# Memory gates that may be projected early, memory values for two token blocks side by side, attention values for two query blocks a group

## The chip, the cores and the metric

The kernel runs on one core of one Trainium2 chip. The metric is the device time of one execution in microseconds (us), as the median of several runs; lower is better. One profiled execution of the same program gives the page and the trace that are read here.

## The reference, cut to what matters

Two layers act on a stream x of 512 tokens by 1024 channels. Each layer has four branches that read the same x: a recurrence (RWKV), a causal attention with low-rank latents (MLA), a convolution, and a cross-attention into 256 memory tokens. Each branch output of width 512 is multiplied by its own gate, projected to 1024 channels and merged under a second set of gates.

```python
h = x @ w_in[l]                                   # all projections of x, gates included
# causal attention, 8 heads of 64, swept in query blocks of 128
s = where(key <= query, (q @ k.T) * scale, -1e30); o = softmax(s) @ v
# memory cross-attention, 4 heads of 128
kv = mem @ w_mem_kv                               # 256 memory tokens: keys and values
y_mem = (softmax(xq @ k_mem.T * scale) @ v_mem) * silu(xg)
...
merged = sum(sigmoid(merge + b) * (y_branch @ w_o_branch), over branches)
x = layer_norm(alpha * x + merged @ w_out)
```

## The kernel before, in words

A product in full precision is made of three matmuls (`mm3`): each operand is split into a high and a low half, and high by low, high by high and low by high are summed in one PSUM bank. A projection of x (`project`) has eight steps over the 1024 input channels, three matmuls of 128 by 512 each, so 24 matmuls. Its weight comes as one DMA of 512 KB, and ScalarE and VectorE split it into halves before TensorE can use it.

Nothing of the order is decided on the chip. While the program is built, the class `Plan` keeps an estimated clock for every engine and lays the instructions out in that order. There are two sources of work. One is a *stream* of items, each with weights to load and a body to run; one item runs at a time and the next waits for it. The other is a set of *tasks* (attention blocks, convolution taps, units of the recurrence), each of which goes on as soon as the planner believes its data to be there. When a task is due it goes first; otherwise the stream gives the next piece; when neither can go on, the planner moves TensorE's clock forward, and the chip will idle there.

- `pick` chooses the next item of the stream: the first in list order whose `ready` holds, and if there is none, the first whose `soon` holds. `prefetch` calls it while fewer than four half-weights are held and fewer than two raw weights are in flight (`LOOK = 4`, `WR = 2`). Weight DMAs are issued by SyncE in that order.
- The list of a layer has latents (`pl`), convolution (`ps_glu`, `ps_val`), memory queries (`ps_xq`), the recurrence's inputs, then four gates and four merge items for each branch. Branch 3 is the memory cross-attention: its gates are `ps_xg` 0 to 3, its merge items give `ps_m` and `po`. A gate item is ready when the branch output that it multiplies exists (`ymem[i]`); a merge item may be taken "soon" once all four gates of its branch have been picked (`picked[n] == 4`), and its body then holds the stream until the four gated outputs `Y[n]` are there. `xq` 2 and 3 are ready when `ymem` 0 and 1 exist.
- Memory values (`pmv`, function `vpart`, by the helper `narrow`): two items a layer, each for 256 value channels. One item computes token block 0 over all eight steps, then token block 1 over the same eight steps; the weights are held through both. `w125` and `w126` are such weights, at the seam of the layers, where layer 0's output is transposed (`xT`), turned into layer 1's x (`xf`, `xh`, `xl`) and read by the latents (`pl`).
- MLA: `pair_item` projects the queries and keys of two heads (`pq`, `pk`), `heads` moves them by DMA to the layout `qT`, `kT`, and `pair` starts eight jobs (`mla_block`), four query blocks for each of the two heads, three in flight at most. A job computes scores (`ms`), maximum (`nmm`), exponential (`mP`), scaling, transposes by TensorE (`mt`) and a copy by ScalarE (`mPT`, four buffers). When both heads of one query block have their `mPT`, their products with the values (`mo`) are issued as one group. These use a 128 by 64 piece of the array, where almost all other matmuls use 128 by 128.
- `Plan.shape` charges the planner's TensorE clock 98 ns whenever the piece of the array changes, and 108 ns more for a return to 128 by 128 unless the matmul is f16. A task that yields "small" waits up to 3 us (`GATHER`) so that small matmuls come together.
- Two PSUM banks belong to the stream (`pp`), two to tasks that use a bank briefly (`pa`), and four to MLA or the recurrence (`pg`).

The recurrence of a layer begins when the four pairs of MLA are done; merge items of the branches fill TensorE beside it.

Of the kernel before, what the change touches and what calls it, by code (L numbers as in the profile page):

```python
# [10 lines left out]
F32 = mybir.dt.float32  # L11
# [14 lines left out]
APART = 150  # L26
ORDER = ["z0", "m0", "m1", "z2", "m2", "m4", "z3", "m3", "m5"]
LOOK = 4
GATHER = 3000.0
WR = 2  # L30
WH = 6
# [40 lines left out]
class Plan:  # L72
# [56 lines left out]
    def shape(self, k, m, quick=False):  # L129


        if (k, m) != self.cut:
            self.clk["PE"] += 98.0 if self.cut != (128, 128) or (k, m) != (128, 128) else 0.0
            if (k, m) == (128, 128) and not quick:
                self.clk["PE"] += 108.0
            self.cut = k, m
            self.cuts += 1
            self.tiled = self.clk["PE"]
# [190 lines left out]
def build(ctx: ExitStack, tc: tile.TileContext, A, out, log, slots, dbg=None):  # L329
# [42 lines left out]
    pp = pool(2, name="pp", space=PSUM)  # L372
    pa = pool(2, name="pa", space=PSUM)
# [141 lines left out]
    both = set()  # L515
# [32 lines left out]
    def free(n=1):  # L548
        wlive["hl"] -= n
# [66 lines left out]
    def narrow(get, cols, blocks, name, lhs, after):  # L616

        wb = []
        for b in range(blocks):
            ps = pp.tile([128, cols], F32, tag="pp", name=f"{name}{b}")  # L620
            for k in range(8):
                if len(wb) <= k // 2:
                    wb.append((yield from get()))
                h, lo = wb[k // 2]
                c = slice(cols * (k % 2), cols * (k % 2) + cols)
                xh, xl = lhs(k, b)
                mm3(ps, xh, xl, h[:, c], lo[:, c], k == 0, k == 7)
                if b == blocks - 1 and k % 2:
                    free()
                if k in (1, 3, 5):  # L630
                    yield
            yield from after(b, ps)
# [26 lines left out]
    def memory_items(l):  # L659

        ms = []
        res = {}

        def load(pool):
            raws = []
            for i in range(4):
                raws.append(u(f"mr{i}_{l}"))
                DMA(raws[i], A["memT"][:, 512 * i:512 * i + 512])
            hl = [[pool(f"mem{n}{i}_{l}") for n in "hl"] for i in range(4)]
            for x in "kv":  # L670
                res[x] = [[u(f"{x}m{n}{i}_{l}", 512, F32R) for n in "hl"] for i in range(2)]
            for i, (h, lo) in enumerate(hl):
                plan.due(raws[i])
                yield
                yield from split(h, lo, raws[i])
                for b in range(2):
                    c = slice(256 * b, 256 * b + 256)
                    ms.append((h[:, c], lo[:, c]))

        def keep(x, i, b, ps):  # L680
            h, lo = (y[:, 256 * b:256 * b + 256] for y in res[x][i])
            return split(h, lo, ps)

        def keys(h):
            def run(get):
                ps = yield from project(get, ms, f"mk{h}_{l}", 256)
                yield from keep("k", h // 2, h % 2, ps)
                yield
            return run

        def vpart(b):
            def after(i, ps):
                yield from keep("v", i, b, ps)
                if b == i == 1:
                    MEM[l] = (res["k"], res["v"])
                yield

            def run(get):
                return narrow(get, 256, 2, f"pmv{b}{l}", lambda k, i: [x[:, 128 * i:128 * i + 128] for x in ms[k]], after)
            return run  # L700

        its = [([(A["w_mk"][l, h], (512, 512))], keys(h)) for h in range(4)]
        its += [([(A["w_mv"][l, b, kh], (512, 512)) for kh in range(2)], vpart(b)) for b in range(2)]
        return load, its, lambda: len(ms) == 8
# [9 lines left out]
    def layer_items(l):  # L714
# [14 lines left out]
        def item(blocks, run, ready=None, picked=None, soon=None):  # L729
            items.append((blocks, run, ready, picked, soon))  # L730

        def ch_item(i, name, after, ready=None, picked=None):

            def run(get):
                ps = yield from project(get, X[l], name + t_)
                after(ps)
                yield
            item([(A["w_ch"][l, i], (512, 512), False, True)], run, ready, picked)

        picked, adds = [0] * 4, [0] * 8  # L740


        if l == 0:
# [775 lines left out]
        def pair(hh, qT, kT, there):  # L1519
            yield lambda: L["turn"] == hh and len(there) == 8  # L1520
            mo, = yield from pg.take([128, 512], f"mo{hh}" + t_)
            plan.t = max(plan.t, *(plan.done[x][0] for x in there + [f"qTpe{hh}1" + t_]))
            yield
            left = [4]
            for i in range(4):
                both = [None, None]
                for h in range(2):
                    while L["jobs"] == 3:
                        yield lambda: L["jobs"] < 3
                    L["jobs"] += 1  # L1530
                    plan.spawn(mla_block(hh, h, i, (qT[h], kT[h]), mo, both, left))
                    yield
            L["turn"] += 1

        def mla_block(hh, h, i, T, mo, both, left):


            n = 128 * i + 128
            dg = slice(128 * i, n)
            q = f"{hh}{h}{i}" + t_  # L1540
            ps, = yield from pg.take([128, n], "ms" + q)
            mm3(ps, *(x[:, dg] for x in T[0]), *(x[:, 0:n] for x in T[1]), True, False)
            MM(ps[:, dg], idb, causal, start=False, stop=True)
            yield
            P = m("mP" + q, 512, "mP", 3)[:, 0:n]
            nm, sm = st("nmm" + q, 1), st("smm" + q, 1)
            V.tensor_reduce(out=nm, in_=ps, axis=AX.X, op=ALU.max, negate=True)
            yield
            S.activation(P, ps, AF.Exp, bias=nm, accum_out=sm)
            pg.free()  # L1550
            yield
            V.reciprocal(sm, sm)
            V.tensor_scalar(out=P, in0=P, scalar1=sm, scalar2=None, op0=ALU.mult)
            yield
            ps, = yield from pg.take([128, n], "mt" + q)
            for kb in range(i + 1):
                TR(ps[:, 128 * kb:128 * kb + 128], P[:, 128 * kb:128 * kb + 128])
            yield
            PT = m("mPT" + q, 512, "mPT", 4)[:, 0:n]
            S.copy(PT, ps)  # L1560
            pg.free()
            both[h] = PT
            L["jobs"] -= 1
            if both[1 - h] is None:
                return
            yield "small"
            for kb in range(i + 1):
                for half, x in zip(range(2), both):
                    MM(mo[HALF[half], dg], vtok[kb][:, 128 * hh + 64 * half:128 * hh + 64 * half + 64], x[:, 128 * kb:128 * kb + 128], start=kb == 0, stop=kb == i)
            left[0] -= 1  # L1570
            if left[0] == 0:
                L["pairs"] += 1
                yield
                yo = u(f"mo{hh}" + t_)
                S.copy(yo, mo)
                pg.free()
                ymla.append(yo)
                if len(ymla) == 4:
                    close_phase()
                    L["mla"] = True  # L1580
# [8 lines left out]
        def gate_items(n, base, name, ready, ys, res, op):  # L1589
            for i in range(4):  # L1590
                def after(ps, i=i):
                    t = sp.tile([128, 512], F32, tag="tg", name=f"t{name}{i}" + t_)
                    S.activation(t, ps, AF.Tanh, scale=0.5)
                    g = u(f"{name}{i}" + t_)
                    V.scalar_tensor_tensor(out=g, in0=t, scalar=1.0, in1=ps, op0=ALU.add, op1=ALU.mult)

                    def fin():
                        yield lambda: ready(i)
                        y = ys[i]
                        op(i, y, g)  # L1600
                        if i == 0:
                            dump(f"y_{name}{l}", y)

                        yield lambda: turn(n)
                        plan.due(y)
                        yield
                        res[i] = yield from halves(f"y{name}{i}", t_, y)
                    plan.spawn(fin())
                def count():
                    picked[n] += 1  # L1610
                ch_item(base + i, f"{name}{i}", after, lambda i=i: ready(i) or n == 0 and added[2] == 8, count)

        def fin(d):
            merged[d] = yield from halves(f"mg{d}", t_, merged[d])
# [462 lines left out]
```

## Time and profile before

| | |
|---|---|
| median of 3 runs | 1527.68 us (1526.68 to 1528.75) |
| the profiled execution | 1528.06 us, its span 1526.3 us |
| TensorE (PE) busy | 1503.4 us, 98% of the span |
| VectorE (DVE) busy | 1079.8 us, 71% |
| ScalarE (ACT) busy | 701.8 us, 46% |
| mean granted TensorE clock | 0.995 |

The span runs from the first to the last instruction; the profiled execution's own time holds 1.8 us more around it. A row of the timeline gives start, duration, engine, line, operation, tiles, shape and count, and in brackets the idle time of the engine ahead of it with what released it. Matmuls overlap, so the price of one is read from start to start, not from its duration. `w147h` is the high half of the stream's weight number 147. A window's row gives the length, then for each engine the busy time and the number of instructions, then the granted TensorE clock (1.00 is full speed), the share of the DMA engines that is busy, and GB/s.

### The profile page before, as it was taken

What the parts mean: (1) busy time and instruction counts of PE and PEld (TensorE: products, weight loads), DVE (VectorE), ACT (ScalarE), POOL (GpSimd) and SP (SyncE); (2) the same over time, 40 slices, a digit from 0 to 9 for tenths busy, and PEclk for the clock granted to TensorE, in tenths of its full rate; (3) what the DMA queues carried; (4) which work ended last, traced back from release to release, by engine and by line L of the source; (5) the groups of instructions that cost most, each with busy time, mean ns of one, the idle gap of its engine ahead of it and who ended that gap; (6) DMA issues with size and microseconds to landing.
All of it is one profiled execution on the core that took longest, in us unless ns stands there. A gap on an engine that the chain in (4) does not pass through costs nothing.

```text
span 1526.3 us, 30171 instructions
## 1 busy us (share of the span) xinstructions
PE 1503.4 (98%) x11942; PEld 1235.8 (81%) x11942; DVE 1079.8 (71%) x2330; ACT 701.8 (46%) x1586; POOL 234.1 (15%) x558
## 2 busy tenths in 40 slices
PE   9999999999999999999999979999999999999997
PEld 9987788877777777888998867788777777778886
DVE  6788887888757774445655878887887777654756
ACT  6546564444345443343364455634544454433330
POOL 0000000334314330000000000000543243300001
PEclk9999999999999999999999999999999999999999
DMA  6351422222222223323343143332222222234222
GB/s 226 126 158 61 107 95 97 74 89 74 72 85 62 76 86 126 110 97 138 115 134 129 53 123 83 109 97 72 88 70 80 86 62 74 86 123 170 97 99 81
DMA packets 69838, 152.13 MB, mean 100 GB/s; under 512 B 24256, under 2 KB 25792, under 8 KB 69696
## 3 DMA queue, kind: packets, MB, share of 16 engines
q1 hardware_dynamic: 69696, 150.20, 31.1%
q8 instruction: 94, 1.54, 0.4%
q14 instruction: 48, 0.39, 0.1%
HBM read 133.39 MB, written 5.24 MB: 91 GB/s over the span
## 4 chain that ended last, share of the span: by engine, by line
PE 94%; DVE 3%; ACT 2%; DMA 1%; issue 0%; SPq 0%; POOL 0%; DVEq 0%; ACTq 0%
PE ps_m L349 23%; PE po L349 11%; PE pz L349 3%; PE ps_xq L349 3%; PE ps_cg L349 3%; PE ps_xg L349 3%; PE ps_rg L349 3%; PE ps_r L349 3%; PE ps_mg L349 3%; PE ps_k L349 3%; PE ps_val L349 3%; PE ps_v L349 3%; PE ps_glu L349 3%; PE ms L349 2%; PE p L349 2%; PE mo L349 1%
## 5 line engine op out<-in xcount | busy, mean ns | idle before, releaser
L269 DVE SCALAR_TENSOR_TENSOR cacc<-hpad,prm,cacc 128x512 f32<-128x512 f32 x240 | 179.5, 750 | 2.9
L269 DVE SCALAR_TENSOR_TENSOR mt<-tm,po 128x512 f32<-128x512 f32 x48 | 32.9, 686 | 125.0 <-PE po L349 110.9
L269 ACT ACTIVATE tm<-ps_m,prm 128x512 f32<-128x512 f32 x64 | 44.1, 690 | 146.4 <-PE ps_m L349 146.0
L269 POOL TENSOR_SCALAR ZT<-W 32x256 f32<-32x256 f32 x16 | 12.7, 792 | 560.0 <-DVE rbl L269 486.6
L269 POOL TENSOR_TENSOR tmpW<-ZT,W 32x14 f32<-32x14 f32 (+6 forms) x224 | 91.2, 407 | 16.3
L269 POOL TENSOR_TENSOR ZT<-ZT,tmpW 32x14 f32<-32x14 f32 (+6 forms) x224 | 88.2, 394 | 17.6
L269 POOL TENSOR_SCALAR gr<-gm 128x4 f32<-128x4 f32 x16 | 5.8, 365 | 237.7 <-DVE gm L269 237.7
L269 ACT ACTIVATE mP<-ms,nmm 128x512 f32<-128x512 f32 (+3 forms) x64 | 33.8, 530 | 12.4 <-DVE nmm L269 11.9
L269 ACT COPY mPT<-mt 128x512 f32<-128x512 f32 (+3 forms) x64 | 27.1, 428 | 21.6 <-PE mt L354 20.9
L269 DVE TENSOR_TENSOR merged<-merged,mt 128x512 f32<-128x512 f32 x48 | 33.4, 697 | 1.7
L354 PE MATMUL mt<-cst,mP 128*128 128x128 f32 x160 | 28.3, 281 | 5.9 <-DVE mP L269 5.9
L269 DVE TENSOR_REDUCE nmm<-ms 128x1 f32<-128x512 f32 (+3 forms) x64 | 30.7, 484 | 4.2 <-PE ms L349 3.6
L269 POOL TENSOR_TENSOR lrs<-lrs,mhalf 128x1 f32<-128x1 f32 x8 | 6.3, 792 | 158.6 <-DVE lrs L269 158.3
L269 POOL TENSOR_SCALAR lrs<-lmv 128x1 f32<-128x1 f32 x4 | 1.5, 370 | 172.6 <-DVE lmv L269 167.0
L354 PEld LDWEIGHTS mt<-cst,mP 128*128 128x128 f32 x160 | 18.8, 142 | 10.9 <-DVE mP L269 6.4
L269 DVE SCALAR_TENSOR_TENSOR S<-w,dpad,H 128x64 f32<-128x64 f32 x48 | 13.4, 279 | 19.7 <-PE w L349 19.6
L269 DVE TENSOR_SCALAR mP<-mP,smm 128x512 f32<-128x512 f32 (+3 forms) x64 | 24.8, 387 | 2.3
L269 ACT COPY R<-p 128x512 f32<-128x512 f32 x32 | 18.9, 590 | 14.8 <-PE p L349 14.8
L349 PE MATMUL mo<-mPT,v 128*64 128x128 f32 x320 | 24.6, 284 | 0.0
L349 PE MATMUL ms<-kTl,qT 96*128 96x512 f32 (+3 forms) x64 | 22.8, 357 | 0.0
L349 PEld LDWEIGHTS mo<-mPT,v 128*64 128x64 f32 x320 | 16.9, 137 | 6.8 <-issue 4.6
L269 ACT ACTIVATE xP<-xs,nmx 128x256 f32<-128x256 f32 x32 | 15.2, 476 | 13.3 <-DVE nmx L269 13.3
(3741 smaller groups left out, 5445.6 us busy)
## 6 DMA issues: line engine op xcount, KB each, us to landing
w<-in_w_ch_dram SPq DMA_DIRECT2D x146, 512.0 KB, 3.8
w<-in_w_o_dram SPq DMA_DIRECT2D x32, 512.0 KB, 3.8
w<-in_w_out_dram SPq DMA_DIRECT2D x16, 512.0 KB, 3.7
w<-in_w_lat_dram SPq DMA_DIRECT2D x16, 336.0 KB, 3.2
w<-in_w_mk_dram SPq DMA_DIRECT2D x8, 512.0 KB, 3.7
w<-in_w_mv_dram SPq DMA_DIRECT2D x8, 512.0 KB, 3.7
w<-in_w_qk_dram SPq DMA_DIRECT2D x8, 320.0 KB, 2.9
x<-in_xT_dram SPq DMA_DIRECT2D x8, 256.0 KB, 5.4
```

The costliest lines, as they stand in the source:

```text
L269: return self.plan.keep(f(*a, **k))
L349: plan.keep(nc.tensor.matmul(o, lhsT, rhs, start=start, stop=stop))
L354: plan.keep(nc.tensor.transpose(o, i, ident))
```

## The change

1. Gates of the memory attention (`n` in `EARLYN`, that is branch 3) get a `soon` condition: they may be taken when nothing is ready, once the attention's latents (`latT`) and the layer's memory keys and values exist, while fewer than `EARLY = 4` gates have been taken before their branch output was ready.
2. `vpart` computes both token blocks step by step, in two PSUM banks (one of `pa`, one of `pp`), and returns a weight when its two steps are done.
3. In MLA the products with the values are issued for two query blocks and two heads at once, four `mPT` to a group, so half as many groups.
4. The planner's charge for a change of the array's piece is 130 ns, before 98 ns. No instruction has this number; only the planner's order can follow from it.

```diff
+EARLY = 4
+EARLYN = 3,
...
-            self.clk["PE"] += 98.0 if self.cut != (128, 128) or (k, m) != (128, 128) else 0.0
+            self.clk["PE"] += 130.0 if self.cut != (128, 128) or (k, m) != (128, 128) else 0.0
...
             def run(get):
-                return narrow(get, 256, 2, f"pmv{b}{l}", lambda k, i: [x[:, 128 * i:128 * i + 128] for x in ms[k]], after)
+                ps = yield from pa.take([128, 256], f"pmv{b}{l}")
+                ps.append(pp.tile([128, 256], F32, tag="pp", name=f"pmv{b}1{l}"))
+                for k in range(8):
+                    if k % 2 == 0:
+                        h, lo = yield from get()
+                    c = slice(256 * (k % 2), 256 * (k % 2) + 256)
+                    for i in range(2):
+                        xh, xl = (x[:, 128 * i:128 * i + 128] for x in ms[k])
+                        mm3(ps[i], xh, xl, h[:, c], lo[:, c], k == 0, k == 7)
+                    yield
+                    if k % 2:
+                        free()
+                for i in range(2):
+                    yield from after(i, ps[i])
+                    if i == 0:
+                        pa.free()
...
-        picked, adds = [0] * 4, [0] * 8
+        picked, adds, early = [0] * 4, [0] * 8, [0]
...
             for i in range(4):
-                both = [None, None]
+                if i % 2 == 0:
+                    both = {}
...
-            both[h] = PT
+            both[i, h] = PT
             L["jobs"] -= 1
-            if both[1 - h] is None:
+            if len(both) < 4:
                 return
             yield "small"
-            for kb in range(i + 1):
-                for half, x in zip(range(2), both):
-                    MM(mo[HALF[half], dg], vtok[kb][...], x[:, 128 * kb:128 * kb + 128], start=kb == 0, stop=kb == i)
-            left[0] -= 1
+            for b in sorted({x for x, _ in both}):
+                dg = slice(128 * b, 128 * b + 128)
+                for kb in range(b + 1):
+                    for half in range(2):
+                        MM(mo[HALF[half], dg], vtok[kb][...], both[b, half][:, 128 * kb:128 * kb + 128], start=kb == 0, stop=kb == b)
+            left[0] -= 2
...
                 def count():
                     picked[n] += 1
-                ch_item(base + i, f"{name}{i}", after, lambda i=i: ready(i) or n == 0 and added[2] == 8, count)
+                    early[0] += not ready(i)
+                def soon():
+                    return n in EARLYN and len(latT) == 5 and MEM[l] is not None and early[0] < EARLY
+                ch_item(base + i, f"{name}{i}", after, lambda i=i: ready(i) or n == 0 and added[2] == 8, count, soon)
```

More of the change, by code (lines that the diff above doesn't have):

```diff
@@ L730, in item, with ch_item @@
             items.append((blocks, run, ready, picked, soon))
-        def ch_item(i, name, after, ready=None, picked=None):
+        def ch_item(i, name, after, ready=None, picked=None, soon=None):
             def run(get):
@@ L737, in run @@
                 yield
-            item([(A["w_ch"][l, i], (512, 512), False, True)], run, ready, picked)
-        picked, adds = [0] * 4, [0] * 8
+            item([(A["w_ch"][l, i], (512, 512), False, True)], run, ready, picked, soon)
+        picked, adds, early = [0] * 4, [0] * 8, [0]
         if l == 0:
@@ L1561, in mla_block @@
             pg.free()
-            both[h] = PT
+            both[i, h] = PT
             L["jobs"] -= 1
-            if both[1 - h] is None:
+            if len(both) < 4:
                 return
             yield "small"
-            for kb in range(i + 1):
-                for half, x in zip(range(2), both):
-                    MM(mo[HALF[half], dg], vtok[kb][:, 128 * hh + 64 * half:128 * hh + 64 * half + 64], x[:, 128 * kb:128 * kb + 128], start=kb == 0, stop=kb == i)
-            left[0] -= 1
+            for b in sorted({x for x, _ in both}):
+                dg = slice(128 * b, 128 * b + 128)
+                for kb in range(b + 1):
+                    for half in range(2):
+                        MM(mo[HALF[half], dg], vtok[kb][:, 128 * hh + 64 * half:128 * hh + 64 * half + 64], both[b, half][:, 128 * kb:128 * kb + 128], start=kb == 0, stop=kb == b)
+            left[0] -= 2
             if left[0] == 0:
```

## The prediction

> **What bounds the kernel now.** I read the page first: is one engine the limit, and how much of the span is it idle?
>
> ```profile
> PE 1503.4 (98%) x11942; PEld 1235.8 (81%) x11942; DVE 1079.8 (71%) x2330; ACT 701.8 (46%) x1586; POOL 234.1 (15%) x558
> PE 94%; DVE 3%; ACT 2%; DMA 1%; issue 0%; SPq 0%; POOL 0%; DVEq 0%; ACTq 0%
> ```
>
> TensorE is busy for 98% of the span, and the chain that ended last is TensorE for 94%. No matmul is removed here, so time can come from three places only: idle TensorE (22.9 us), a TensorE at a lower clock, or the price of changing the piece of the array. Next the waits of TensorE:
>
> ```profile
> PE mt L354 <- DVE mP L269: 5.9, 1, 5.9
> PE pmv L349 <- DVE w125l L269: 1.5, 1, 1.5
> PE ps_val L349 <- DVE xql L269: 1.4, 1, 1.4
> PE xs L349 <- ACT xy L269: 1.3, 1, 1.3
> PE pmv L349 <- DVE w126l L269: 0.6, 1, 0.6
> PE pk L349 <- DVE xkl L269: 0.5, 1, 0.5
> ```
>
> One wait stands out, 5.9 us for one transpose. Third, windows: the stages of the two recurrences, layer 1's MLA, and the place of that wait (the last four rows were asked for TensorE alone).
>
> ```profile
> 253.00:575.00 322.00, 321.57 (x3588) 254.69 (x3587) 241.43 (x558) 149.97 (x342) 108.96 (x262) 1.00 0.25 78
> 883.00:903.00 20.00, 12.35 (x64) 9.75 (x63) 16.33 (x40) 9.60 (x29) 0.00 (x0) 0.83 0.62 155
> 903.00:992.00 89.00, 87.59 (x573) 68.53 (x571) 73.70 (x166) 52.98 (x145) 0.00 (x0) 1.00 0.33 97
> 1030.00:1350.00 320.00, 320.00 (x3592) 253.40 (x3591) 241.38 (x560) 150.48 (x341) 109.37 (x262) 1.00 0.25 77
> 877.40:886.60 9.20, 8.73 (x40) 1.00 0.36 87
> 891.00:895.80 4.80, 0.24 (x3) 1.00 0.96 281
> 895.80:902.60 6.80, 5.44 (x23) 0.50 0.27 55
> 776.33:779.74 3.41, 3.12 (x14) 0.50 0.13 50
> ```
>
> In the recurrences TensorE is never idle; from 883 to 903 us it lacks 7.65 us of 20, a third of all its idle time, and then works at half clock until 902.6. That is the start of layer 1's MLA. Fourth, its timeline:
>
> ```profile
> 891.01 0.23 PE L349 MATMUL ms<-causal,idb 128*128 128x128 bf16 x1
> 897.16 0.47 PE L354 MATMUL mt<-cst,mP 128*128 128x128 f32 x1 [5.92 <-DVE mP L269]
> 901.46 0.78 PE L349 MATMUL ps_xq<-xl,w147h 128*128 128x512 f32 x1
> 890.45 1.07 SPq L361 DMA_DIRECT2D w<-in_w_ch_dram  x2
> 897.83 0.62 ACT L269 CAST w147h<-w 128x512 fp32r<-128x512 f32 x1
> ```
>
> The stream had nothing: its next weight, 147, is loaded at 890.45, split from 897.83 and used at 901.46. It is memory query 3, ready only when `ymem` 1 exists. The gates 1 to 3 were also waiting for their outputs. So TensorE stands behind the first `mP`.
>
> **1. Early gates.** While pairs 0 and 1 are projected (877.4 to 886.6), `pick` found nothing; now it finds gates. The price of one:
>
> ```profile
> L349 PE MATMUL ps_xg<-xl,w151h x8: 389/389/499, 944.8 to 949.5; 128*128 128x512 f32 x8
> L349 PE MATMUL ps_xg<-xh,w151l x8: 389/389/393, 945.9 to 950.2; 128*128 128x512 f32 x8
> ```
>
> 24 matmuls from 944.8 to 950.2, with the last one 5.6 us. Two gates (11.2 us) cover the 7.65 us. What a gate brings along: a weight DMA of 0.53 us on SyncE's queue (1.07 for two), two casts of 0.62 us on ScalarE and two subtractions on VectorE, at the end one activation and one product, all of 128 by 512 and so of about the same length. These move from 897 to 905 to before the hole. The DMA engines are then 36% busy, while from 891 to 895.8 they are 96% busy with these two weights and pair 1's copies; so the move costs nothing, and if VectorE's cover were gone it would be 2 us on `mP`, already late. Gate results live longer in SBUF, at no time.
>
> What comes back: of the idle time, the 5.92 us wait is what a gate can fill. The 1.3 us of `xs` and 0.5 us of `pk` are matmuls that are themselves late; a gate behind them does not help, so they stay. The order is fixed by the planner's clock, and a transpose laid out too early stands in front of its gate as before. I leave 1.2 us of the 5.92 for this (the other waits for late data are 1.3, 1.4 and 1.5 us) and take 4.7 us. The half clock covers 5.44 us of matmuls that would take 2.72: another 2.7 us. Term: -7.4 us; bounds 0 (filled nowhere) and -7.65 - 2.7 = -10.35.
>
> Here a rule of the Trainium skill can be weighed. The row first: at the seam of the layers the clock was also 0.50 for 3.41 us (776.33 to 779.74), after waits of only 1.50 and 0.62 us. By "TensorE: Matmul & The Clock Gate", Part 1, the clock is halved after at least one idle window of about 3.4 us; then a rest of 1.2 us would keep the full clock and the 2.7 us come back whole. By the seam's row such a rest may still cost one window, 3.41 / 2 = 1.7 us, and the term would be -5.7. The measurement decides that short waits can cost a window.
>
> In layer 0 TensorE has no such hole; a gate taken early only swaps places: 0.
>
> **2. Memory values side by side.** The matmuls are the same; what changes is how much work a half-weight gives before the next is needed: twelve matmuls, before six.
>
> ```profile
> 774.58 0.39 PE L349 MATMUL pmv<-w125l,memh 128*128 128x256 f32 x1 [1.50 <-DVE w125l L269]
> 776.62 0.58 PE L349 MATMUL pmv<-w126l,memh 128*128 128x256 f32 x1 [0.62 <-DVE w126l L269]
> 796.87 0.69 DVE L269 TENSOR_TENSOR xl<-xf,xh 128x512 fp32r<-128x512 f32 x1 [0.83 <-ACT xh L269]
> 797.97 0.32 PE L349 MATMUL pl<-w130l,xh 128*128 128x336 f32 x1
> ```
>
> Six more matmuls of 256 columns, at half of the 5.6 / 24 = 0.23 us that one of 512 takes above, are 0.7 us of cover ahead of each half, so the waits of 1.50 and 0.62 us shrink to about 0.8 and nothing, and the half clock (1.7 us) may go. But what is late next is x: the last of its eight pieces ends at 797.56 and the latents read it at 797.97, so only 0.4 us can be had unless the transposes, which stand behind the same waits in TensorE's queue, come earlier too. I take twice that, -0.8 us; bounds 0 and -(1.50 + 0.62 + 1.7) = -3.8. The other three places have no wait on weights: 0. The two block copies now come together at the end, and `pmv` holds a bank of `pa`; memory queries and transposes ahead of it cover that, and without cover it would be one copy of ScalarE and VectorE, about 0.8 us an item, inside the range.
>
> **3. Values for two query blocks a group.** 31 groups of `mo` (two of the 32 run together), the first at 119.40, the last at 990.93:
>
> ```profile
> 119.40 0.44 PE L349 MATMUL mo<-mPT,v 128*64 128x128 f32 x4
> 149.63 0.40 PE L349 MATMUL pq<-lth,w28l 128*128 128x512 f32 x1
> 149.96 1.09 PE L349 MATMUL mo<-mPT,v 128*64 128x128 f32 x16
> 150.98 0.50 PE L349 MATMUL pq<-ltl,w28h 128*128 128x512 f32 x1
> 151.55 0.39 PE L349 MATMUL pq<-lth,w28l 128*128 128x512 f32 x1
> 990.60 0.40 PE L349 MATMUL ps_mg<-xh,w155l 128*128 128x512 f32 x1
> 990.93 1.09 PE L349 MATMUL mo<-mPT,v 128*64 128x128 f32 x16
> 992.41 0.39 PE L349 MATMUL ps_mg<-xh,w156h 128*128 128x512 f32 x1
> ```
>
> Twelve more matmuls cost 1.09 - 0.44 = 0.65 us, 0.054 each, so sixteen are 0.87. From 149.63 to 151.55 are 1.92 us; less 0.87 and three matmuls of 0.23 leaves 0.36 us for the two changes of piece. In the second group the return is by an f16 matmul: 992.41 - 990.60 = 1.81, less the same, leaves 0.25. Many groups stand next to attention matmuls, where it is nearer the lower, so I take 0.25. 16 groups instead of 31: 15 x 0.25 = -3.8 us (TensorE is 98% busy there, so it counts). Bounds: -5.4 (0.36 each) and 0, if the longer wait of the early blocks gives it back.
>
> **4. The planner's charge.** No instruction. The order shifts a little everywhere; in the recurrences, with 0.43 us idle of 642, there is nothing to gain and something to lose. I take 0, from -0.4 to +2 us (two waits of the size of 1 us).
>
> **Sum.** -7.4 - 0.8 - 3.8 = -12.0 us, from the profiled execution's 1528.06: 1516.1, which I round to 1516. The median shown, 1527.68, is 0.4 lower and changes nothing beside the range. All best ends: 1528.06 - 10.35 - 3.8 - 5.4 - 0.4 = 1508.
>
> **Rivals.**
>
> *A. The hole is half filled.* VectorE is busy for 16.33 of the 20 us and the wait for `mP` ended only at 897.16. If the planner believes it done after half a gate, TensorE runs one and waits as before. With 3 us and one half-clock window (1.7) left in place of 1.2 and none, the sum is 3.5 worse: about 1520.
>
> *B. The gates are spent before the hole,* between 853 and 877, where `pick` may also find nothing. Then terms 2 and 3 remain: 1523.5. Against it: four gates, and the hole needs two.
>
> *C. The gates open the door to the merge too soon.* Once all four are picked, `soon` of the first merge item holds, long before `Y[3]`; its body then holds the stream.
>
> ```profile
> L349 PE MATMUL ps_xq<-xh,w147l x8: 390/396/468, 902.5 to 915.8; 128*128 128x512 f32 x8
> L349 PE MATMUL xo<-xPTh,vml x4: 389/392/397, 909.3 to 940.1; 128*128 128x512 f32 x4
> L349 PE MATMUL ps_xg<-xl,w148h x8: 392/476/577, 918.2 to 931.5; 128*128 128x512 f32 x8
> L349 PE MATMUL ps_glu<-xl,w149h x8: 389/396/578, 932.7 to 940.3; 128*128 128x512 f32 x8
> ```
>
> From the last matmul of query 3 (915.8) to `Y[3]` (940.1, a copy, a product and a split: 943) are 27.2 us, nearly all busy now. Two projections of the stream lie in them (11.2 us) and the start of a third item (about 2), so 14 are attention. With one merge gate as the only stream (5.6 us), some 7.5 us are idle, and one or two half-clock windows add 1.7 to 3.4: about 10 us, and 1526, no change. For it: nothing in `soon` asks for the outputs. Against it: convolution items and the next pair become ready in that time and go first.
>
> *D. Slower: the larger group holds ScalarE.* A group takes all four `mPT`, so the next copy waits until its values are done; 28 matmuls (blocks 2 and 3) are 1.5 us, and behind it in ScalarE's queue stand the next exponentials and weight casts. If this reaches TensorE with 1.0 us in each of 16 groups, the time is 1516 + 16 = 1532; it decides from 12 + 3 over 16, 0.94 us a group. Against it: copies come one every 2.3 us.
>
> ```profile
> L269 ACT COPY mPT<-mt x12: 260/479/597, 903.8 to 928.9; 128x384 f32<-128x384 f32 x4, 128x256 f32<-128x256 f32 x3, 128x512 f32<-128x512 f32 x3, 128x128 f32<-128x128 f32 x2
> ```
>
> **How the numbers follow.** Forecast 60% (1510 to 1519), A 12%, B 6%, C 12%, D 10%. Predicted 1516. The range 1510 to 1526 holds the forecast, A and B and the edge of C. About 0.2% (3 us) is what a measurement of this kernel tells from no change: faster is the forecast with A and B, 78%; C is the same, 12%; D is slower, 10%.
>
> **What would show it.** Right: `ps_xg` matmuls between the first `ms` and the first `mt` of layer 1, the wait of 5.9 us gone or under 2, the clock 1.00 from 890 to 905; 16 groups of `mo` with 12 and 28 matmuls; no wait on `w126l` in `pmv`, and `pl` waiting for x at the seam. Wrong: the same wait of `mt` behind a gate (A), four `ps_xg` ahead of 877 (B), `ps_m` of branch 3 in layer 1 followed by idle TensorE (C), ScalarE's `mPT` waiting for `mo` (D), or a new wait in a recurrence (term 4).

## The result, and the profile after

The median after is 1517.1 us (1515.1 to 1518.8, 6 runs) against 1527.7 us (1526.7 to 1529.6, 6 runs): a ratio of 0.9928, interval 0.9915 to 0.9941, so 10.6 us less. The forecast was 1516. The profiled execution took 1517.33 us with a span of 1515.5, 10.8 less than the span before. The sum was nearly right, in part by luck: its first term was wrong in two places, with opposite signs.

First the page of the changed kernel (busy times, chain), then its waits of TensorE:

```profile
PE 1499.9 (99%) x11942; PEld 1238.6 (82%) x11942; DVE 1077.7 (71%) x2330; ACT 698.8 (46%) x1581; POOL 232.6 (15%) x558
...
PE 96%; DVE 2%; DMA 1%; ACT 1%; issue 0%; SPq 0%; POOL 0%; DVEq 0%; ACTq 0%
```

```profile
PE mt L356 <- DVE mP L271: 2.7, 1, 2.7
PE pmv L351 <- DVE w125l L271: 1.1, 1, 1.1
...
PE mt L356 <- DVE smm L271: 0.9, 2, 0.5
```

The same 11942 matmuls; TensorE idles for 15.6 us, before 22.9. The wait of 5.9 us is gone, and so are those of `xs` (1.3), `pk` (0.5), `ps_val` (1.4) and `w126l` (0.6). But there is a new wait for `mP`, 2.7 us. To see where it stands, I cut the span at two instructions that both programs have, the first of the seam (`ps_mk`) and the first after it (`ps_glu`); two rows of before, then two of after:

```profile
768.79 0.29 PE L349 MATMUL ps_mk<-meml,w124h 128*128 128x256 f32 x1
...
814.53 0.39 PE L349 MATMUL ps_glu<-xl,w135h 128*128 128x512 f32 x1
```

```profile
771.60 0.29 PE L351 MATMUL ps_mk<-meml,w124h 128*128 128x256 f32 x1
...
815.11 0.39 PE L351 MATMUL ps_glu<-xl,w135h 128*128 128x512 f32 x1
```

| stretch | before | after | difference |
|---|---|---|---|
| layer 0, to `ps_mk` | 768.79 | 771.60 | +2.8 |
| seam, to `ps_glu` | 45.74 | 43.51 | -2.2 |
| layer 1, to the end of the span | 711.77 | 700.39 | -11.4 |

Layer 0 became slower although it has half the groups; layer 1 gained more than was forecast for it.

**Layer 1.** Windows of the changed kernel (columns as before), and then its gates, pair 0 and query 3 as groups of equal instructions:

```profile
883.00:903.00 20.00, 19.95 (x108) 16.71 (x108) 16.68 (x40) 11.49 (x30) 0.00 (x0) 1.00 0.66 172
903.00:1002.00 99.00, 97.91 (x625) 78.85 (x623) 83.96 (x183) 57.07 (x152) 0.00 (x0) 1.00 0.33 95
1035.00:1355.00 320.00, 320.00 (x3603) 253.65 (x3601) 242.27 (x565) 148.93 (x341) 107.48 (x262) 1.00 0.25 77
```

```profile
L351 PE MATMUL ps_xg<-xl,w145h x8: 393/397/486, 877.9 to 883.3; 128*128 128x512 f32 x8
...
L351 PE MATMUL pq<-ltl,w146h x3: 389/395/396, 885.3 to 887.4; 128*128 128x512 f32 x3
...
L351 PE MATMUL ps_xq<-xl,w148h x8: 389/392/478, 893.9 to 900.5; 128*128 128x512 f32 x8
```

From 883 to 903 us TensorE is busy for 19.95 of 20 us at the full clock, before 12.35 at 0.83. The gate does not stand between the first scores and the first transpose, as I had it: it stands at 877.9, where pair 0 began before (877.4), and pair 0 moves to 885.3. By the time the pairs' scores are out, query 3 has become ready, and its matmuls (893.9 to 901) cover the wait for `mP`.

**Layer 0.** The new hole in the timelines of TensorE, ScalarE and SyncE's queue, and then the windows around it:

```profile
177.42 0.39 PE L351 MATMUL ps_xq<-xh,w33l 128*128 128x512 f32 x1
180.49 0.33 PE L356 MATMUL mt<-cst,mP 128*128 128x128 f32 x1 [2.69 <-DVE mP L271]
```

```profile
178.37 0.62 ACT L271 CAST w34h<-w 128x512 fp32r<-128x512 f32 x1 [7.72 <-DMA w<-in_w_ch_dram]
178.89 0.36 ACT L271 ACTIVATE mP<-ms,nmm 128x128 f32<-128x128 f32 x1
```

```profile
172.58 0.58 SPq L363 DMA_DIRECT2D w<-in_w_ch_dram  x1
```

```profile
174.00:178.00 4.00, 3.81 (x23) 2.97 (x22) 1.54 (x4) 0.00 (x0) 0.00 (x0) 1.00 0.95 262
178.00:182.00 4.00, 1.51 (x6) 1.17 (x7) 2.91 (x9) 2.94 (x10) 0.00 (x0) 0.86 1.06 225
180.87:184.28 3.41, 3.41 (x12) 2.71 (x11) 2.67 (x6) 1.27 (x6) 0.00 (x0) 0.50 0.78 233
```

The releaser named for `mt` is VectorE, but the bracket on ScalarE tells the cause: it stood for 7.72 us before the cast of weight 34, whose DMA had not landed, and the exponential that makes `mP` stands behind that cast in its queue. The DMA engines are 95% busy from 174 to 178 us. A half-clock window of 3.41 us follows, in which about 1.7 us of time are lost.

### The profile page after: what moved, and what is told of

It is laid out like the page before. It is cut to its first block, busy times and chain, and to the rows that moved or that the text cites. A ratio compares the mean times of both kernels' runs of the same rounds, so it can differ in the third digit from the quotient of the medians.

```text
span 1515.5 us, 30180 instructions
## 1 busy us (share of the span) xinstructions
PE 1499.9 (99%) x11942; PEld 1238.6 (82%) x11942; DVE 1077.7 (71%) x2330; ACT 698.8 (46%) x1581; POOL 232.6 (15%) x558
## 4 chain that ended last, share of the span: by engine, by line
PE 96%; DVE 2%; DMA 1%; ACT 1%; issue 0%; SPq 0%; POOL 0%; DVEq 0%; ACTq 0%
PE ps_m L351 23%; PE po L351 12%; PE pz L351 3%; PE ps_cg L351 3%; PE ps_xg L351 3%; PE ps_mg L351 3%; PE ps_k L351 3%; PE ps_rg L351 3%; PE ps_v L351 3%; PE ps_r L351 3%; PE ps_val L351 3%; PE ps_xq L351 3%; PE ps_glu L351 3%; PE ms L351 2%; PE pl L351 2%; PE p L351 2%
## 5 line engine op out<-in xcount | busy, mean ns | idle before, releaser
L271 ACT ACTIVATE mP<-ms,nmm 128x128 f32<-128x128 f32 (+3 forms) x64 | 33.7, 530 | 13.4 <-DVE nmm L271 12.0
L271 ACT COPY mPT<-mt 128x128 f32<-128x128 f32 (+3 forms) x64 | 27.2, 428 | 20.8 <-PE mt L356 14.7
L271 DVE TENSOR_REDUCE nmm<-ms 128x1 f32<-128x128 f32 (+3 forms) x64 | 30.3, 484 | 2.1 <-PE ms L351 1.9
L271 POOL TENSOR_SCALAR lrs<-lmv 128x1 f32<-128x1 f32 x4 | 1.5, 368 | 172.6 <-DVE lmv L271 167.2
L271 DVE TENSOR_SCALAR mP<-mP,smm 128x128 f32<-128x128 f32 (+3 forms) x64 | 24.8, 387 | 2.3
L271 ACT CAST rbh<-w 128x256 fp32r<-128x256 f32 x16 | 6.5, 406 | 39.8 <-DVE w L271 39.7
L351 PE MATMUL ms<-kTl,qT 96*128 96x128 f32 (+3 forms) x64 | 22.3, 349 | 0.0
L351 PE MATMUL mo<-mPT,v 128*64 128x128 f32 x320 | 21.0, 278 | 0.0
```

The costliest lines, as they stand in the source:

```text
L271: return self.plan.keep(f(*a, **k))
L351: plan.keep(nc.tensor.matmul(o, lhsT, rhs, start=start, stop=stop))
```

## Experiments

Each was timed in five rounds beside the kernel before: e1 to e4 on one chip, e5 to e8 on a second and e9 to e12 on a third (the kernel before took 1527.84, 1528.23 and 1527.87 us there). "Ratio" is to that kernel. The intervals are about 2 us to each side for e6 to e12, so differences of 1 to 2 us between those runs are read together with the traces.

| run | median us | ratio, interval |
|---|---|---|
| e1 gates alone | 1519.61 | 0.9946 (0.9934 to 0.9959) |
| e2 values alone | 1526.66 | 0.9990 (0.9982 to 0.9999) |
| e3 groups alone | 1525.73 | 0.9985 (0.9976 to 0.9993) |
| e4 charge alone | 1529.32 | 1.0011 (1.0002 to 1.0020) |
| e5 after, without gates | 1524.41 | 0.9975 (0.9965 to 0.9985) |
| e6 after, gates in layer 1 only | 1513.21 | 0.9902 (0.9888 to 0.9915) |
| e7 after, charge 98 | 1513.57 | 0.9902 (0.9887 to 0.9917) |
| e8 after, small groups | 1517.73 | 0.9936 (0.9922 to 0.9949) |
| e9 after, one load on another queue | 1518.79 | 0.9931 (0.9918 to 0.9945) |
| e10 e6 with charge 98 | 1514.68 | 0.9913 (0.9899 to 0.9926) |
| e11 e6 with small groups | 1519.40 | 0.9944 (0.9931 to 0.9956) |
| e12 e6 with narrow values | 1513.99 | 0.9909 (0.9895 to 0.9922) |

**Which part gives what: e1 to e4.** Each is the kernel before with one of the four parts. My theory: the parts add up, and the gates are the main one. The rival: any shift of the planner's order removes the wait of 5.9 us.

```diff
+    def soon():                                       # e1: part 1 of the change
+        return n in EARLYN and len(latT) == 5 and ...
-    return narrow(get, 256, 2, f"pmv{b}{l}", ...)     # e2: part 2
+    mm3(ps[i], xh, xl, h[:, c], lo[:, c], k == 0, k == 7)
-    if both[1 - h] is None:                           # e3: part 3
+    if len(both) < 4:
-    self.clk["PE"] += 98.0 if ...                     # e4: part 4
+    self.clk["PE"] += 130.0 if ...
```

> The kernel before with the early gates alone (memory values, attention groups and the planner's charge as before). Theory 1, the gates fill the hole: in layer 1 the wait of a transpose for mP (5.9 us before) and the half-clock stretch behind it (6.8 us) are gone, worth about 10 us; in layer 0 two gates are laid in front of pairs 2 and 3, and the 2.7 us wait near 177 us with its half-clock window, as the changed kernel shows it, comes with them, about -4.5 us. Sum: 6 us faster, ratio about 0.996. Rival 2, the hole went because the attention groups changed: then the wait of 5.9 us is still there and the time is 1527 to 1529.

> The kernel before with the memory values side by side alone. Theory 1: one wait on w125l of about 1.1 us, none on w126l, no half clock at the seam of the layers, so 2.2 us faster from the seam (the seam's stretch from the last memory key to the end of the latents takes 43.4 us in the changed kernel and 45.6 before); layer 1's wait for mP stays near 6 us. Ratio about 0.9986. Rival 2, the seam is held by the eight pieces of x: 0.4 us faster at most. Had re-planning alone been the cause of the gain, layer 1's wait would go here too.

> The kernel before with the attention values for two query blocks a group alone. Theory 1: 16 groups of mo instead of 31, 0.25 us each, so 3.8 us faster, ratio about 0.9975, and layer 1's wait for mP stays. Rival 2: the wait goes with the groups and the time is about 1517, ratio 0.993. Rival 3, a group holds all four mPT and ScalarE waits for it: 0 to 5 us slower, ScalarE's mPT waiting for mo in the chain of waits.

> The kernel before with the planner's charge of 130 ns alone. Theory 1: no instruction changes, only the order; within 2 us of before, ratio 0.9987 to 1.0013, layer 1's wait for mP still 4 us or more. Rival 2, any new order removes that wait: 5 us or more faster.

Against a before of 1527.84 us the four give -8.2, -1.2, -2.1 and +1.5: together -10.0, where the whole change gave -10.6. The waits of TensorE, first of e2, then of e3, then of e4:

```profile
PE mt L356 <- DVE mP L271: 5.8, 1, 5.8
```

```profile
PE mt L356 <- DVE mP L271: 5.9, 1, 5.9
...
PE zw L351 <- DVE yr L271: 1.0, 1, 1.0
...
PE mo L351 <- ACT mPT L271: 1.0, 2, 0.5
```

```profile
PE mt L354 <- DVE mP L269: 5.9, 1, 5.9
...
PE gk_1x L354 <- DVE B L269: 0.9, 1, 0.9
```

All three orders differ from that of before, and the wait stays: the rival falls, the gates remove it. e1 was 2 us faster than expected: the hole in layer 0 that was expected in it is not there (its transposes wait 0.36 us near 178 us). In e2 the seam became 1.9 us shorter and keeps the full clock, near the 2.2 us expected, but the half-clock stretch at layer 1's hole lasts 10.24 us in place of 6.83, and the whole is 1.2 us faster. In e3 the groups save what they should, but three new waits of 0.5 to 1.0 us take half of it back, two of them the wait for `mPT` that rival D described, only twice and not sixteen times. In e4 a wait of 0.9 us opens in a recurrence.

**The parts taken out or reduced in the changed kernel: e5 to e8.** The question was the loss in layer 0.

```diff
-EARLYN = 3,                                             # e5
+EARLYN = ()
-    return n in EARLYN and len(latT) == 5 and ...       # e6
+    return l == 1 and n in EARLYN and len(latT) == 5 and ...
-    self.clk["PE"] += 130.0 if ...                      # e7
+    self.clk["PE"] += 98.0 if ...
-    if len(both) < 4:                                   # e8, with the loops of before
+    if both[1 - h] is None:
```

> The changed kernel with the early gates taken out again; the other three parts stay. Theory (the parts add up, and the gates are the main one): the wait of about 5.8 us of a transpose for mP in layer 1 comes back with a half-clock stretch behind it, and the time is 8 us above the changed kernel's, about 1525. Rival (beside the other parts the gates lose 4.5 us in layer 0: the hole of 2.85 us at 177 us of the changed kernel's trace and a half-clock window of 3.41 us, 1.7 us of work, behind it): that hole goes with them, and the time is only 4 us above, about 1521.

> The changed kernel with the early rule in layer 1 alone. Theory (the hole at 177 us comes from the two gates taken early in layer 0): the hole of 2.85 us and the half-clock window of 3.41 us behind it are gone, layer 1 is as in the changed kernel, and the time is 4 to 4.5 us below it, about 1513. Rival (the hole comes from the larger groups or the charge, since the gates alone did not show it): the hole stays, and the time is within 1 us of 1517.

> The changed kernel with the planner's charge for a change of piece back at 98. Theory (the charge alone cost 1.5 us and this adds to the rest): about 1515.6, and the hole at 177 us stays. Rival (the charge shifts the order of layer 0 so that the hole opens there): the hole and its half-clock window go, and the time is about 1512.5. Second rival (there is nothing but chance in the charge, as the prediction had it): within 1 us of 1517 with other small waits.

> The changed kernel with attention values again one query block a group (32 groups). Theory (the groups add to the rest): 3.7 us more price at the changes of piece, less about 1.6 us of waits that the larger groups made when they were alone, so about 1519. Rival (the larger groups hold the mP and mPT buffers in layer 0 and open the hole at 177 us): 3.7 us dearer and 4.5 us cheaper, about 1516.

e5: 7.3 us above the changed kernel; its wait is back (5.9 us), with a half-clock stretch of 6.83 us, and the hole of layer 0 is gone. e6: 3.9 us below it, as the theory said, with no half clock before the end of the span; with this charge and these groups, early gates in layer 0 cost time and those in layer 1 carry the whole gain. Where pairs 2 and 3 are projected in layer 0, in the changed kernel and in e6:

```profile
L351 PE MATMUL pq<-ltl,w30h x3: 389/389/389, 162.7 to 164.0; 128*128 128x512 f32 x3
...
L351 PE MATMUL pq<-ltl,w31h x3: 397/397/496, 166.3 to 167.8; 128*128 128x512 f32 x3
```

```profile
L351 PE MATMUL pq<-ltl,w28h x3: 387/397/478, 148.1 to 151.8; 128*128 128x512 f32 x3
...
L351 PE MATMUL pq<-ltl,w31h x3: 397/397/475, 170.7 to 172.2; 128*128 128x512 f32 x3
```

Two gates taken early keep pair 2 from the stream until 162.7, and then pair 3 is ready too: the pairs lie 3.6 us apart, in e6 22.6 us, and their sixteen copies and a weight meet in the DMA engines. The DMA queue between 167 and 179 us (packets, MB, share of the 16 engines), in the changed kernel and in e6:

```profile
q1 hardware_dynamic: 1276, 2.38, 82.0%
```

```profile
q1 hardware_dynamic: 428, 0.93, 29.2%
```

e7 and e8 met neither expectation alone. In e7 (3.5 us below) the pairs lie 3.7 us apart and the hole is there, but with a wait of 0.9 us and no half clock: load 34 is issued at 170.97 us and its cast starts at 176.94, 1.4 us earlier than above. In e8 the other order puts the pairs 11.3 us apart (155.9 and 167.2), and there is no hole at this place; it is 0.6 us above the changed kernel, since 15 more groups cost about what the hole did. So the gates push the pairs towards each other, and the rest of the order decides how close they come and how deep the hole is.

That the two bursts meet is not yet the price. In e1 the pairs lie 4.0 us apart and in e7 3.7, and in both the DMA engines are 97% busy between 167 and 179 us, more than the 82% above; yet the transposes wait 0.36 and 0.86 us there and not 2.69. What differs is when pair 2's copies go out. SyncE's queue in the changed kernel, and then in e1:

```profile
166.91 0.51 SPq L363 DMA_DIRECT2D qTl<-qrl  x1
167.51 1.18 SPq L363 DMA_DIRECT2D qT<-xqh  x2
```

```profile
165.68 1.14 SPq L363 DMA_DIRECT2D qT<-xqh  x2
...
170.72 0.58 SPq L363 DMA_DIRECT2D w<-in_w_ch_dram  x1
```

In the changed kernel the first operand of these copies (`xqh`) is written by 165.52 us, but ahead of them in the queue stands an earlier copy of rotated queries (`qTl` from `qrl`). By the profile it waited for VectorE's split of gate 1's product (`yxg1l`, 166.16 to 166.84). So the copies start at 167.51 us, in e1 at 165.68 and in e7 at 165.94, and the load of weight 34 behind them at 172.58, 170.72 and 170.97. In all three its cast starts 5.8 to 6.0 us after that. The hole is deeper by about what the queue is late. This is read from three traces; no run moved that one copy.

**Queue or engines: e9.** The load of weight 34 stands in SyncE's queue behind eight pair copies. Is it the queue that makes it late, or the engines?

```diff
-        DMA(raw, src)
+        DMA(raw, src, other=name == "w34")     # gpsimd.dma_start for this one
```

> The changed kernel with one instruction moved: the load of weight 34 is issued on GpSimd's queue in place of SyncE's. The instructions of TensorE, VectorE and ScalarE and their order are the same. Theory (the hole at 177 us is SyncE's queue: the load stands behind eight pair copies and is issued only at 172.58, and the cast of this weight at 178.37 stands in ScalarE's queue ahead of the exponentials that make mP): the load goes out soon after its buffer is free, near 167.5, the cast runs before 175, the wait of 2.7 us for mP and the half-clock window behind it are gone, and the time is 4 us below the changed kernel's, about 1513. Rival (the DMA engines are the limit, busy for 89 to 95% from 170 to 178 us): the load lands about as late as before, or the copies land later by as much, and the time stays within 1.5 us of 1517.

The theory was wrong; the waits of TensorE, the cast of weight 34 on ScalarE, and the issues of the DMAs between 167 and 179 us (queue, count, KB, median us to landing):

```profile
PE ms L351 <- DMA kTl<-xkl: 2.8, 1, 2.8
```

```profile
173.98 0.62 ACT L271 CAST w34h<-w 128x512 fp32r<-128x512 f32 x1 [3.32 <-DMA w<-in_w_ch_dram]
```

```profile
w<-in_w_ch_dram POOLq DMA_DIRECT2D x1, 512.0 KB, 6.2
...
kTl<-xkl SPq DMA_DIRECT2D x4, 128.0 KB, 5.8
```

The load went out at 167.75 us and its cast ran 4.4 us earlier, as expected, and the wait for `mP` is gone. But the copies of `kTl`, issued at nearly the same times, took 5.8 us in place of 3.3: they share the DMA engines with the load. This agrees with the Trainium skill, "Trainium Kernel Development and Optimization", Key Constraints: DMAs from the SyncE, ScalarE and GpSimd queues all share the same 16 DMA engines, and a second queue saves only issue time. The scores themselves now wait for these copies, 2.8 us. The hole moved from `mt` to `ms` and kept its size, and behind it the clock is halved for 6.83 us. The median is 1.7 us above the changed kernel's, just outside the 1.5 us of the rival. So moving this load alone gains nothing; that the queue has no part is not shown, since the first copies still start at 167.51 us here.

**What the other parts are worth without the hole: e10 to e12.** Each is e6 with one part undone.

```diff
-    self.clk["PE"] += 130.0 if ...                      # e10
+    self.clk["PE"] += 98.0 if ...
-    if len(both) < 4:                                   # e11
+    if both[1 - h] is None:
-    ps = yield from pa.take([128, 256], f"pmv{b}{l}")   # e12
+    return narrow(get, 256, 2, f"pmv{b}{l}", ...)
```

> The changed kernel with the early rule in layer 1 alone and the charge back at 98. Theory (in the changed kernel the charge of 130 cost time only by making the hole of layer 0 deeper, 2.85 against 1.03 us, and its half-clock window): with that hole gone the charge is worth nothing, and the time is 1513, as with 130. Rival (the 1.5 us that the charge cost alone adds to everything): about 1511.7.

> The changed kernel with the early rule in layer 1 alone and attention values one query block a group, so that no hole of layer 0 blurs the price of the groups. Theory (16 groups more at about 0.24 us of start-to-start loss each, less up to 1.6 us of waits that belong to the larger groups): 2 to 3.8 us above 1513.2, about 1516. Rival (the waits of the larger groups give their whole gain back): within 0.5 us of 1513.2.

> The changed kernel with the early rule in layer 1 alone and memory values one token block at a time again. Theory (the two waits of 1.5 and 0.6 to 1.4 us at the seam come back in place of one of 1.1): 1 to 1.5 us above 1513.2, and about 1.7 more if a half-clock window follows them. Rival (x is late there anyway, so that the waits only move): within 0.5 us of 1513.2.

e10: 1.5 us above e6, with intervals that overlap; in layer 0 a transpose waits 0.9 us for `mP` again. Neither expectation held. A charge of 130 for 98 was worth +1.5 us (e4), +3.5 (against e7) and -1.5 (against e10): the sign depends on the rest of the order, as a charge that no instruction pays would have it. e11: 6.2 us above e6, more than expected. Here too I summed, for every group, the time from start to start around it less what the same matmuls take in a run: about 7 us for its 30 groups, about 4 for the 16 of e6. That is some 3 of the 5.6 us between the two profiled spans (1516.5 and 1510.9); TensorE idles as long in both (14.8 and 14.5 us). Of the 5.6 us 4.7 lie in layer 0, ahead of `ps_mk`; what makes up the rest of them stays unexplained. e12: 0.8 us above e6, between its two expectations and less than the intervals. e6 is the best version here by its median, with e7, e10 and e12 inside the intervals; no run of e6 or e7 is as slow as the fastest of the changed kernel (1515.06 us).

**Early gates in layer 0, from four bases.** The runs give one more comparison. Of each pair below, one program has early gates in layer 0 and the other has none there; the charge and the groups are the same. The figures are the start of the same `ps_mk` (weight 124) in each trace, in us, so the length of layer 0:

| charge, query blocks a group | without | with | difference |
|---|---|---|---|
| 98, one | before, 768.79 | e1, 768.96 | +0.2 |
| 98, two | e10, 768.73 | e7, 767.60 | -1.1 |
| 130, one | e11, 770.89 | e8, 768.71 | -2.2 |
| 130, two | e6, 766.16 | changed kernel, 771.60 | +5.4 |

The medians agree in sign where they can be compared: e7 is 1.1 us below e10 and e8 1.7 below e11 (both inside the intervals), the changed kernel 3.9 above e6. So early gates in layer 0 are not dear in themselves; they cost time only where the charge of 130 and the larger groups come with them. Each figure is one execution.

## Why the prediction was right, and where it was not

**Term 1, early gates: -7.4 forecast; -8.2 alone (e1), -7.3 when taken out (e5).** In the changed kernel it came out right in sum by luck, through two errors of opposite sign; e1 has only the first of them.

- In layer 1 it was too cautious. Not 4.7 but all of the 5.92 us went, and the 2.7 of the half clock. "They stay" was said of `xs` (1.3) and `pk` (0.5); both went, since the gate came ahead of the pairs and not between scores and transpose. Together 10.4, the best end of the term's range. New waits of `mt` for `smm` (0.9 us in two) take some back. With half of term 3 (1.9) the forecast for this layer was -9.3; measured -11.4.
- "In layer 0 a gate taken early only swaps places: 0" is the step that failed in this kernel. What it swaps places with is a pair, and a pair brings eight copies of 128 KB. The working counted the DMAs that a gate brings along and not those of the work that it delays. Price: 2.7 us of wait and 1.7 of half clock, 4.4; by e6, 3.9 us. On the three other bases of the table the 0 held or was even too cautious (+0.2, -1.1, -2.2 us): the price belongs to gates, groups and charge together, and why just these three parts meet so badly is read from the traces, not tested.

**The clock rule.** The prediction let the seam's row decide against the rule that it cites, and the row was the better guide: a wait of 2.69 us cost one window of 3.41. But short waits do not always cost one. In e1 the seam has the same two waits as before and a third, and the clock stays at 1.00:

```profile
774.74 0.38 PE L351 MATMUL pmv<-w125l,memh 128*128 128x256 f32 x1 [1.50 <-DVE w125l L271]
...
776.78 0.39 PE L351 MATMUL pmv<-w126l,memh 128*128 128x256 f32 x1 [0.65 <-DVE w126l L271]
...
778.99 0.39 PE L351 MATMUL pmv<-w126l,memh 128*128 128x256 f32 x1 [0.79 <-DVE w126l L271]
```

```profile
771.00:784.00 13.00, 10.02 (x79) 9.12 (x78) 6.59 (x13) 9.64 (x18) 0.81 (x1) 1.00 0.58 192
```

**Term 2, memory values: -0.8 forecast; -1.2 (e2), -0.8 (e12).** The seam of the changed kernel is 2.2 us shorter, but there the half-clock window is gone as well, which e1 shows to go without this part. Its waits:

```profile
777.38 0.39 PE L351 MATMUL pmv<-w125l,memh 128*128 128x256 f32 x1 [1.08 <-DVE w125l L271]
```

The wait of 1.50 shrank to 1.08 and not to 0.8, and that on `w126l` is gone. By the medians the term was sized right. By the seam alone it was too small: with the full clock on both sides the seam takes 45.4 us in e12 and 43.7 in e6. The prediction held x to be late next; but x came earlier too. Its last piece `xl` starts 28.1 us after `ps_mk` before and 26.4 us after it in the changed kernel, and the expected wait of `pl` for x did not show.

**Term 3, groups: -3.8 forecast; -2.1 (e3), -0.6 (against e8), -6.2 (against e11).** The groups are 16, of 12 and 28 matmuls; the last:

```profile
1000.51 1.75 PE L351 MATMUL mo<-mPT,v 128*64 128x128 f32 x28
```

The price of 0.25 us a group held: summed as above, about 8 us for the 31 groups before and about 4 for the 16 after, so about 0.25 each and some 4 us saved. (The 128 by 128 matmuls around them are those of the attention's stage; over the whole program 4800 of the 11942 matmuls use 64 by 64, nearly all others 128 by 128.) What the forecast lacked is that a new order brings other small losses, for better or worse by 2 us and more, as e3, e8 and e11 show.

**Term 4, the charge: 0 forecast, -0.4 to +2.** +1.5 alone (e4), inside the bounds. In the changed kernel it is 3.5 us (e7), where the hole in layer 0 is deep enough for a half-clock window; that meeting of gates, groups and charge no term had.

**Rivals.** A and B did not come: the hole of layer 1 is wholly filled, and two of the four gates were spent early there, at 865 and 877.9. C came in its path and not in its price: the first merge item of branch 3 is taken as soon as the gates are picked (`ps_m` of weight 151, 933.3 to 940.9 us) and runs without idle time. D is in e3 and e5, twice 0.5 us each, and not in the changed kernel.

## What to carry to other kernels

When an item is pulled forward, ask what it pushes back, which transfers that work brings, and what stands ahead of them in their queue; a queue of an engine that holds a cast of a late weight ahead of critical work turns a late transfer into idle TensorE. Try a rule only where the hole is: here in layer 1 alone, 1513.2 us, though with the old charge both layers did as well (e7, 1513.6). In an order laid out by a planner, every edit reshuffles small waits by one to three us, so a part's own worth is told from several bases, not from one run.

## What the runs showed of the hardware that was not expected

The half-clock stretches away from the end of the span last 3.41, 6.83 or 10.24 us (the last in e2, 889.05 to 899.29), one, two or three times 3.413, and the two of before (776.33 and 895.79) start 119.46 us apart, 35 times it: they lie on a grid of windows. Whether a wait costs a window seems to differ from run to run of one kernel. Of the five runs of e9 one took 1514.88 us at a mean granted clock of 0.999, the others 1517.36 to 1519.76 at 0.996 and 0.997; only the slowest has a trace, with 6.83 us at half clock. That the position of the wait on the grid decides is inferred, not shown; the Trainium skill, "TensorE: Matmul & The Clock Gate", Part 1, says that the window runs freely and that its phase varies from run to run, which agrees.
